# Two transformer blocks on one core: the retrieval's decode for four token tiles at once, with a selection by bits

## The chip, the cores and the metric

The kernel runs on one core of a Trainium2 chip. Its engines work side by side, each with a queue of its own in order: TensorE (PE, with its weight loads as PEld), VectorE (DVE), ScalarE (ACT), GpSimd (POOL) and SyncE (SP), which issues most transfers. The metric is the device time of one execution in microseconds; the median of the runs counts.

## The reference, cut to what matters

512 tokens of 1024 features pass two blocks of a transformer. The first has a mixer of attention and RWKV heads and a gated feed-forward network; the second has HGRN2 and retention heads and then PEER, a layer that retrieves its experts. The change touches PEER alone:

```
q = (h @ w_q).reshape(T, 8 heads, 2 halves, 128)
s = einsum('thpd,hpkd->thpk', q, sub_keys)          # 128 sub-keys for each (head, half)
top_s, top_i = top_k(s, 16)
cand = top_s[:, :, 0, :, None] + top_s[:, :, 1, None, :]
cand_idx = top_i[:, :, 0, :, None] * 128 + top_i[:, :, 1, None, :]
best_s, best_c = top_k(cand.reshape(T, 8, 256), 16)
expert_idx = take_along_axis(cand_idx.reshape(T, 8, 256), best_c, axis=-1)
gates = softmax(best_s, axis=-1)
out[t] = sum over the 128 chosen of gates * gelu(expert_u[idx] . h[t]) * expert_v[idx]
```

There are 128 x 128 experts, so an expert is a pair of sub-keys (i, j).

## The kernel before, in words

Products are exact in float32: each operand is split in a high and a low part, and a product is three TensorE passes (`mm3`). Weights come through a ring of tiles of 128 x 1024 (`_load` on SP's queue, `_split`: the high part is a ScalarE copy, L238, and the low part a subtraction, L241). While the retrieval and the gate matrix run, `pool_split` is 1 and all low parts are made on POOL. The ring splits three tiles ahead.

The instructions of each engine are put in order by a planner when the program is built, after a model of time; an engine then runs its own list strictly in that order and waits where an operand is late. Sections with `high_priority` are pulled forward, and `issue_after` holds a piece behind another.

PEER has four token tiles of 128 tokens. For the first three, all experts are computed: for each j, the product of the 128 rows (., j) of expert_u with the tokens (`expert_act`), gated and multiplied with expert_v. For tile 3, the chosen rows are gathered from DRAM by POOL's indirect DMA (`gather_rows`). The order of `peer` is:

- `retrieve`, for groups hp of two heads (four products c of a head and half each): the product with w_q (`gemm_fm`), ScalarE's copy q, the scores `psc` on TensorE, ScalarE's copy `sc`; then for each tile `top16` on VectorE (five instructions: eight largest, their places, replace, and again, 16 in all). After each pair of halves, POOL adds the candidates of a tile (`cand`, 64 + 48 columns of the pairs that can be chosen) and VectorE finds their best 16 (`bs`, their places `bc`). When the group's four products are through, `decode` runs once for each tile: softmax of the scores into `gate`, the place in `bc` taken apart into the two places a and b (shifts, masks, casts to float and a predicated copy for candidates from 64 on), and then the sub-key at that place. For the latter a table lookup is made of an equality with 0 to 15 (VectorE, L1306, 128 x 512), a product with the 16 sub-key numbers (POOL, L1307) and a sum (VectorE, L1308) into `sel`.
- the gates and sub-keys of the three dense tiles are transposed (`slots_T`), and `gate_matrix` builds each token's 128 x 128 matrix of gates from two one-hots, `ohA` (VectorE) and `ohB` (VectorE or POOL), with TensorE (`pg`) and a ScalarE copy, and writes it to DRAM (`gd`).
- 25 of the 40 early `expert_act` products (L264 to L266 with `acc`) stand in the program between retrieval and gate matrix, and the planner may place them in TensorE's gaps; the last 15 run among the gate matrix's steps. Then follows the loop over all 128 j.

Of the kernel before, what the change touches and what calls it, by code (L numbers as in the profile page):

```python
# [57 lines left out]
TILES = (3, 0, 1, 2)  # L58
# [31 lines left out]
def prep(inp):  # L90
    """Lays the inputs out; every array is a permutation, slice or stack of inputs, or depends on shapes alone."""
# [77 lines left out]
# ---------------------------------------------------------------- program  # L169
class Prog:  # L170
# [26 lines left out]
    def banks(self, spec):  # L197
        """spec: "bank name name; ..." """
# [24 lines left out]
    # ring of weight tiles  # L223
# [44 lines left out]
    def gemm_fm(self, X, M=128, bank="acc", parts=1):  # L268
        """one block of 128 output features x 512 tokens; X: list of (hi, lo) FM chunks"""
# [42 lines left out]
    def split(self, src, name):  # L312
        """FM f32 chunk in SBUF -> exact parts"""
# [8 lines left out]
    # constants  # L322
    def consts(self):
# [12 lines left out]
        self.iota16 = self.iota[:, 0:16]  # L336
        # derived per-channel vectors
# [13 lines left out]
        # lower bound: softmax over the two rows, first row  # L351
# [8 lines left out]
        # f = lb + (1 - lb) (tanh / 2 + 1/2) = tanh * c1 + c0  # L360
# [7 lines left out]
    def attn_consts(self):  # L368
        """constants of the first mixers only"""
# [18 lines left out]
    def first_loads(self):  # L388
        """tokens, the first gain and the first weights in the order of their use"""
# [29 lines left out]
    def rstd_of(self, ss, n, eps, w=1):  # L419
        """(ss / n + eps) ** -0.5 of a small tile"""  # L420
# [7 lines left out]
    def new_U(self):  # L428
        """8 FM chunks of exact parts"""
# [4 lines left out]
    def rstd_row(self, ss):  # L434
        """(sum + eps) ** -0.5 of the two scaled square sums of a row"""
# [6 lines left out]
    def square(self, x, ss):  # L442
        """sum of squares / D along the row"""
# [3 lines left out]
    def norm_tile(self, i, gb, banks=("C", "D"), ss=None):  # L447
        """rmsnorm of one token tile of self.X, into its columns of the FM chunks; ss: with its first square sum"""
# [24 lines left out]
    def norm_fm(self, gb):  # L473
        """rmsnorm of self.X as 8 FM chunks of exact parts"""
# [44 lines left out]
    # ------------------------------------------------------------ block 1  # L519
# [10 lines left out]
    def lat_part(self, U):  # L530
# [19 lines left out]
        # forget gates of the attention heads: rows 32..39  # L550
# [18 lines left out]
    def fox_proj(self, c, U):  # L569
        """queries, keys and values of two heads"""  # L570
# [84 lines left out]
    def rwkv_elem(self, c):  # L655
        """two heads of the RWKV group on 128 channels"""
# [5 lines left out]
        # decay  # L662
# [15 lines left out]
        # in-context rate  # L678
# [9 lines left out]
        # normalised key  # L688
# [16 lines left out]
        # gate and bonus  # L705
# [41 lines left out]
        # [b k] scaled to the end of their chunk, tokens on partitions  # L747
# [9 lines left out]
        # rows: even head (b; k), odd head: transposed from (k; b)  # L757
# [4 lines left out]
        # scores  # L762
# [18 lines left out]
        # values, tokens on partitions  # L781
# [9 lines left out]
    def rwkv_inv(self, e, g_, h):  # L791
        """(I - N)^-1 of two chunks by doubling"""
# [878 lines left out]
```

## Time and profile before

| | us |
|---|---|
| median of 3 runs | 3137.03 |
| the three runs | 3127.26, 3137.03, 3152.71 |
| span of the profiled execution | 3129.2 |
| TensorE busy in it | 2961.4 (95%) |
| VectorE busy | 1938.7 (62%) |
| ScalarE busy | 1228.4 (39%) |
| POOL busy | 1508.5 (48%) |

The profiled execution has no time of its own beside its span, from its first to its last instruction. Busy shares are means over stages of different kinds; the rows below cut the span into stages. In a row, `cuf<-cm,cuf` means that tile cuf is written from tiles cm and cuf, `128x512` is partitions by elements of each, and a line Lnnn is that of kernel.py. In a wait, the part behind `<-` is what ended it.

### The profile page before, as it was taken

The numbers are of one execution on the slowest core, as the hardware profiler recorded it, in microseconds if no ns is written. First come the engines' busy times: TensorE is split into PE (matmuls) and PEld (weight loads), VectorE is DVE, ScalarE is ACT, GpSimd is POOL, SyncE is SP. The second block draws the span as 40 slices with busy tenths as digits, with TensorE's granted clock in tenths as the row PEclk, the third lists the DMA queues.
The fourth block names the chain that finished last, engine by engine and source line by source line (L and its number), as shares of the span: only waits on it lengthen the run. The fifth ranks groups of instructions, "written<-read, shape, count | busy, mean of one in ns | idle before, by whom it ended". The sixth has DMA issues, their size and how long they took to land.

```text
span 3129.2 us, 40869 instructions
## 1 busy us (share of the span) xinstructions
PE 2961.4 (95%) x15129; PEld 2547.7 (81%) x15129; DVE 1938.7 (62%) x3421; ACT 1228.4 (39%) x1925; POOL 1508.5 (48%) x1150
## 2 busy tenths in 40 slices
PE   7999898999999999999999978888999999999998
PEld 6877787888878878888888868887888888888876
DVE  4247755443135653555423899997777777787788
ACT  5455644222243433444423324565333333333333
POOL 3222213222245652333323457866767677667665
PEclk9998999999999999999999989999999999999999
DMA  4120013333332213222333223446888988888886
GB/s 156 56 68 8 1 38 109 97 98 97 95 113 69 62 47 101 85 85 85 90 116 123 92 68 95 142 169 219 297 275 293 308 289 298 299 280 299 285 310 240
DMA packets 174359, 473.65 MB, mean 151 GB/s; under 512 B 15056, under 2 KB 64592, under 8 KB 172624
## 3 DMA queue, kind: packets, MB, share of 16 engines
q1 hardware_dynamic: 137296, 336.80, 33.8%
q0 software_dynamic: 36864, 134.23, 12.2%
q8 instruction: 120, 1.97, 0.3%
q14 instruction: 79, 0.65, 0.1%
HBM read 439.49 MB, written 31.46 MB: 151 GB/s over the span
## 4 chain that ended last, share of the span: by engine, by line
PE 69%; DVE 15%; DMA 7%; issue 5%; ACT 2%; POOL 1%; SPq 0%; DVEq 0%; POOLq 0%; ACTq 0%
PE acc L266 13%; PE acc L265 13%; PE acc L264 13%; DMA urow<-ev,ei 3%; PE A L266 3%; PE A L264 3%; PE A L265 3%; PE B L266 3%; PE B L265 3%; PE B L264 3%; DMA urow<-eu,ei 2%; PE pg L1377 2%; DVE lo L241 2%; PE i L804 1%; PE lev L981 1%
## 5 line engine op out<-in xcount | busy, mean ns | idle before, releaser
L241 POOL TENSOR_TENSOR lo<-raw,hi 128x1024 fp32r<-128x1024 f32 x278 | 689.6, 2481 | 912.9 <-ACT hi L238 875.8
L238 ACT ACTIVATE hi<-raw 128x1024 fp32r<-128x1024 f32 x501 | 529.3, 1057 | 1065.7 <-PE acc L265 441.4
L266 PE MATMUL acc<-u,lo 128*128 128x512 f32 (+3 forms) x2344 | 864.6, 369 | 39.2 <-DVE lo L241 21.2
L264 PE MATMUL acc<-u,hi 128*128 128x512 f32 (+3 forms) x2344 | 862.4, 369 | 15.0 <-ACT x L1392 6.3
L265 PE MATMUL acc<-u,hi 128*128 128x512 f32 (+3 forms) x2344 | 862.1, 368 | 0.7 <-DVE u L471 0.7
L266 PEld LDWEIGHTS acc<-u,lo 128*128 128x128 f32 (+1 forms) x2344 | 448.1, 191 | 96.2 <-DVE lo L241 27.6
L264 PEld LDWEIGHTS acc<-u,hi 128*128 128x128 f32 (+1 forms) x2344 | 447.8, 191 | 70.0 <-ACT eact L1392 6.7
L265 PEld LDWEIGHTS acc<-u,hi 128*128 128x128 f32 (+1 forms) x2344 | 448.3, 191 | 54.8 <-issue 2.7
L241 DVE TENSOR_TENSOR lo<-raw,hi 128x1024 fp32r<-128x1024 f32 x223 | 304.4, 1365 | 301.1 <-ACT hi L238 299.9
L1332 DVE SCALAR_TENSOR_TENSOR urow<-urow,h4row 128x1024 f32<-128x1024 f32 x128 | 201.5, 1595 | 109.2 <-DMA urow<-eu,ei 108.9
L1342 DVE SCALAR_TENSOR_TENSOR po<-urow,act,po 128x1024 f32<-128x1024 f32 x127 | 203.2, 1600 | 84.9 <-DMA urow<-ev,ei 83.5
L1324 POOL DMA_INDIRECT urow<-eu,ei x128 | 193.5, 1512 | 32.6 <-issue 19.0
L1324 POOL DMA_INDIRECT urow<-ev,ei x128 | 176.6, 1380 | 37.8 <-issue 18.2
L1403 ACT ACTIVATE wh<-wf 128x384 fp32r<-128x384 f32 x128 | 67.1, 525 | 272.3 <-PE D L265 243.5
L1368 DVE TENSOR_SCALAR ohA<-iota,slT 128x128 f32<-128x128 f32 x384 | 129.8, 404 | 0.9 <-PE pg L1377 0.7
L1377 PE MATMUL pg<-ohB,ohA 128*128 128x128 f32 x768 | 106.3, 280 | 25.0 <-DVE ohB L1374 12.5
L1377 PEld LDWEIGHTS pg<-ohB,ohA 128*128 128x128 f32 x768 | 97.4, 191 | 32.7 <-ACT gstage L1379 16.1
L1379 ACT ACTIVATE gstage<-pg 128x512 f32<-128x512 f32 x96 | 99.5, 1089 | 57.8 <-PE pg L1377 57.7
L1372 POOL TENSOR_SCALAR ohB<-iota,slT 128x128 f32<-128x128 f32 x144 | 98.2, 698 | 39.9 <-PE pg L1377 39.7
L266 PE MATMUL A<-hi,wl 128*128 128x512 f32 x256 | 95.8, 399 | 10.0 <-DVE wl L1404 9.9
L265 PE MATMUL A<-lo,wh 128*128 128x512 f32 x256 | 101.0, 395 | 0.8 <-POOL lo L241 0.8
L264 PE MATMUL A<-hi,wh 128*128 128x512 f32 x256 | 99.8, 390 | 0.6 <-ACT wh L1403 0.6
(539 smaller groups left out, 5395.9 us busy)
## 6 DMA issues: line engine op xcount, KB each, us to landing
raw<-ut SPq DMA_DIRECT2D x128, 512.0 KB
raw<-ev SPq DMA_DIRECT2D x128, 512.0 KB
raw<-w_ret SPq DMA_DIRECT2D x48, 512.0 KB
gd<-gstage SPq DMA_DIRECT2D x12, 2048.0 KB
gread<-gd SPq DMA_DIRECT2D x32, 768.0 KB
raw<-w_gu SPq DMA_DIRECT2D x44, 512.0 KB
raw<-w_hg SPq DMA_DIRECT2D x32, 512.0 KB
raw<-w_in SPq DMA_DIRECT2D x27, 512.0 KB
```

Source lines behind the costliest of these rows:

```text
L238: self.nc.scalar.activation(hi, raw, AF.Copy)
L241: r = eng.tensor_tensor(lo, raw, hi.bitcast(F32), op=ALU.subtract)
L264: mm(out, a[0], b[0], start=start, stop=False)
L265: mm(out, a[0], b[1], start=False, stop=False)
L266: return mm(out, a[1], b[0], start=False, stop=stop).ins
L1324: r = nc.gpsimd.indirect_dma_start(out=u, out_offset=None, in_=src, in_offset=bass.IndirectOffsetOnAxis(ap=ei[:, s:s + 1], axis=0))
L1332: nc.vector.scalar_tensor_tensor(u, u, 1.0, row, op0=ALU.mult, op1=ALU.mult, accum_out=act[:, s:s + 1])
L1342: nc.vector.scalar_tensor_tensor(o, u, act[:, s:s + 1], o, op0=ALU.mult, op1=ALU.add)
L1368: nc.vector.tensor_scalar(A4[:, r], self.iota, sl[:, 0, k + r:k + r + 1], sl[:, 2, k + r:k + r + 1], op0=ALU.is_equal, op1=ALU.mult)
L1372: nc.gpsimd.tensor_scalar(B4[:, r], self.iota, sl[:, 1, k + r:k + r + 1], None, op0=ALU.is_equal)
L1377: last = nc.tensor.matmul(p[:, r, :], A4[:, r], B4[:, r], start=True, stop=True)
L1379: nc.scalar.activation(st[:, :, q * 4:q * 4 + 4].rearrange("p j t -> p t j"), p, AF.Copy)
```

## The change

The tiles of the retrieval get a dimension for the four token tiles, and `decode` runs once for each group of two heads on all four: four times in place of sixteen. POOL's two candidate sums run on all four tiles at once as well; `top16` stays one call for each tile and product, now in the order 0 to 3. The place of a candidate stays an integer. The lookup no longer compares, multiplies and sums: the 16 sub-key numbers (`tif`, now cast by ScalarE) are halved step by step. ScalarE spreads the lower eight over the 16 slots (`mux`, 128 x 2048); VectorE then, for the bits 8, 4, 2 and 1 of the place, masks the bit and copies the upper half of what is left over the lower half where the bit is set. ScalarE copies what remains into `sel`. The gates of the gathering tile get a copy of their own (`gate3`), since the retrieval's tiles are freed. Comments and docstrings go too.

```diff
-                for i in TILES:
-                    self.top16(ts[i][:, c, :], ti[i][:, c, :], s[:, i, :], 128)
+                for i in range(4):
+                    self.top16(ts[:, i, c, :], ti[:, i, c, :], s[:, i, :], 128)
                 if c % 2:
-                    for i in TILES:
-                        t0, t1 = ts[i][:, c - 1, :], ts[i][:, c, :]
-                        cand = self.b("cand", [128, 112])
-                        nc.gpsimd.tensor_tensor(cand[:, 0:64].rearrange("p (a b) -> p a b", b=16),
...
-                        self.top16(bs[i][:, c // 2, :], bc[i][:, c // 2, :], cand, 112)
-            for i in TILES:
-                self.decode(i, hp, ti[i], bs[i], bc[i])
+                    t0, t1 = ts[:, :, c - 1, :], ts[:, :, c, :]
+                    cand = self.b("cand", [128, 4, 112])
+                    for o, a, nb in ((0, slice(0, 4), 16), (64, slice(4, 16), 4)):
+                        na = a.stop - a.start
+                        nc.gpsimd.tensor_tensor(cand[:, :, o:o + na * nb].rearrange("p i (a b) -> p i a b", b=nb),
+                                                t0[:, :, a, None].to_broadcast([128, 4, na, nb]),
+                                                t1[:, :, None, 0:nb].to_broadcast([128, 4, na, nb]), op=ALU.add)
+                    for i in range(4):
+                        self.top16(bs[:, i, c // 2, :], bc[:, i, c // 2, :], cand[:, i, :], 112)
+            self.decode(hp, ti, bs, bc)
+        self.gate3 = self.b("gate3", [128, 8, 16])
+        nc.scalar.activation(self.gate3, self.gate[:, 3], AF.Copy)
...
+        ab = self.b("ab", [128, 4, 2, 2, 16], U32)
+        tail, u, f = self.b("cm", B2, U32), self.b("cu", B2, U32), self.b("cuf", B2)
         TS(tail, bc, 64, None, op0=ALU.is_ge)
-        for w in range(2):
-            uf = []
-            for n in range(2):
-                u = self.b("cu", B3, U32)
...
-            nc.vector.copy_predicated(uf[0], tail, uf[1])
-            eq = self.b("eq", B4)
-            TT(eq, uf[0][:, :, :, None].to_broadcast(B4), self.iota16[:, None, None, :].to_broadcast(B4), op=ALU.is_equal)
-            nc.gpsimd.tensor_tensor(eq, eq, tif[:, :, w, None, :].to_broadcast(B4), op=ALU.mult)
-            nc.vector.tensor_reduce(self.sel[i][w][:, H, :], eq, axis=AX.X, op=ALU.add)
+        TS(u, bc, 2, None, op0=ALU.logical_shift_right)
+        nc.vector.tensor_copy(f, u)
+        TS(f, f, -12.0, None, op0=ALU.add)
+        nc.vector.tensor_copy(u, f)
+        TS(ab[:, :, :, 0, :], bc, 4, None, op0=ALU.logical_shift_right)
+        nc.vector.copy_predicated(ab[:, :, :, 0, :], tail, u)
+        u = self.b("cu", B2, U32)
+        TS(u, bc, 3, None, op0=ALU.bitwise_and)
+        TS(ab[:, :, :, 1, :], bc, 15, None, op0=ALU.bitwise_and)
+        nc.vector.copy_predicated(ab[:, :, :, 1, :], tail, u)
+
+        tif = self.b("tif", [128, 16, 16])
+        nc.scalar.activation(tif, ti.rearrange("p i c k -> p (i c) k"), AF.Copy)
+        w = self.b("mux", [128, 16, 16, 8])
+        nc.scalar.activation(w, tif[:, :, None, 0:8].to_broadcast([128, 16, 16, 8]), AF.Copy)
+        n = 8
+        while n:
+            bit = self.b("bit", [128, 16, 16], U32)
+            TS(bit, ab.rearrange("p i h two k -> p (i h two) k"), n, None, op0=ALU.bitwise_and)
+            B4 = [128, 16, 16, n]
+            nc.vector.copy_predicated(w[:, :, :, 0:n], bit[:, :, :, None].to_broadcast(B4),
+                                      tif[:, :, None, 8:16].to_broadcast(B4) if n == 8 else w[:, :, :, n:2 * n])
+            n //= 2
+        w = w.rearrange("p (i h two) k e -> p i h two k e", h=2, two=2)
+        for j in range(2):
+            nc.scalar.activation(self.sel[j][:, :, H, :], w[:, :, :, j, :, 0], AF.Copy)
...
-        P.open(eq1, "retrieve", "xs 10 gb keys q sc; eq 4 junk; ts 8; ti 8; bs 8; bc 8; wk 3; cand 3; tif 4; cm 4; cu 4; cuf 8; ef 1; gate 3; sel0 4; sel1 4")
+        P.open(eq1, "retrieve", "xs 10 gb keys q sc; mux 1; ts 2; ti 2; bs 2; bc 2; wk 3; cand 2; tif 1; ab 1; bit 2; cm 1; cu 2; cuf 1; ef 1; gate 1; sel0 1; sel1 1")
```

The softmax at the head of `decode` keeps its five instructions, on four tiles each. A number behind a tile's name in the last two lines is its count of buffers: the retrieval's tiles of a group now have two, those inside `decode` mostly one.

## Rows read from the trace of the kernel before

**Rows 1.** The page's first line.

```profile
span 3129.2 us, 40869 instructions
```

**Rows 2.** Four stages; columns: length, busy us and instructions by engine, clock, DMA share, GB/s.

```profile
1743.60:1862.00 118.40, 106.36 (x523) 90.94 (x522) 117.08 (x634) 36.39 (x57) 62.23 (x63) 0.94 0.24 72
1862.00:1979.00 117.00, 89.28 (x460) 86.19 (x460) 116.30 (x474) 42.49 (x58) 84.26 (x69) 0.90 0.29 86
1979.00:2162.00 183.00, 158.31 (x1118) 150.89 (x1117) 175.81 (x439) 117.95 (x126) 136.93 (x158) 1.00 0.48 177
2162.00:3129.00 967.00, 925.97 (x4511) 819.90 (x4509) 732.65 (x774) 326.74 (x456) 658.43 (x374) 0.99 0.85 288
```

**Rows 3.** Chain of waits by line, 1743 to 1985, then 1985 to 2165 us.

```profile
by line: DVE wk L1228 9.7%; DVE eq L1306 8.6%; DVE sel L1308 6.8%; DVE ti L1230 6.6%; DVE ti L1226 6.6%; DVE cuf L1304 5.3%; DVE cu L1298 4.8%; DVE ts L1225 4.8%; DVE ts L1229 4.7%; DVE cuf L1303 4.2%; DVE tif L1287 3.6%; DVE gate L1280 3.4
...
by line: PE pg L1377 32.8%; DVE ohA L1368 11.7%; DVE ohB L1374 11.0%; PE acc L266 10.9%; PE acc L264 10.8%; PE acc L265 10.8%; issue 8.3%; ACT gstage L1379 3.7%; ACT eact L1392 0.1%; ACTq L1379 0.0%
```

**Rows 4.** VectorE's groups by line, 1743 to 1980 us: busy us, mean ns; idle before.

```profile
L1306 DVE TENSOR_TENSOR eq<-cuf,iota 128x512 f32<-128x512 f32 x32 | 25.2, 822 | 0.0
L1308 DVE TENSOR_REDUCE sel<-eq 128x32 f32<-128x512 f32 x32 | 21.4, 672 | 0.6 <-POOL eq L1307 0.6
...
L1304 DVE COPY_PREDICATED cuf<-cm,cuf 128x32 f32<-128x32 uint32 x32 | 15.5, 488 | 0.0
...
L1298 DVE TENSOR_SCALAR cu<-bc 128x32 uint32<-128x32 uint32 x32 | 13.7, 450 | 0.0
L1303 DVE TENSOR_SCALAR cuf<-cuf 128x32 f32<-128x32 f32 x16 | 11.5, 721 | 0.0
L1300 DVE CAST cuf<-cu 128x32 f32<-128x32 uint32 x64 | 10.5, 206 | 0.0
L1287 DVE CAST tif<-ti 128x64 f32<-128x64 uint32 x16 | 10.0, 640 | 0.0
L1280 DVE TENSOR_TENSOR gate<-bs 128x32 f32<-128x32 f32 x16 | 9.6, 598 | 0.0
...
L1296 DVE TENSOR_SCALAR cu<-bc 128x32 uint32<-128x32 uint32 x32 | 8.7, 286 | 0.0
...
L1285 DVE TENSOR_TENSOR gate<-gate,gsum 128x32 f32<-128x32 f32 x16 | 7.1, 446 | 0.0
...
L1290 DVE TENSOR_SCALAR cm<-bc 128x32 uint32<-128x32 uint32 x16 | 5.1, 320 | 0.0
```

**Rows 5.** VectorE in order of time: start us, length us.

```profile
1893.21 0.16 DVE L1290 TENSOR_SCALAR cm<-bc 128x32 uint32<-128x32 uint32 x1
1893.29 0.26 DVE L1296 TENSOR_SCALAR cu<-bc 128x32 uint32<-128x32 uint32 x2
```

**Rows 6.** One line or tile: least, middle, largest ns; first and last start us.

```profile
L1306 DVE TENSOR_TENSOR eq<-cuf,iota x32: 668/682/2901, 1783.3 to 1971.9; 128x512 f32<-128x512 f32 x32
...
L1308 DVE TENSOR_REDUCE sel<-eq x32: 661/673/687, 1791.5 to 1977.3; 128x32 f32<-128x512 f32 x32
...
L1304 DVE COPY_PREDICATED cuf<-cm,cuf x32: 175/190/2429, 1779.8 to 1968.6; 128x32 f32<-128x32 uint32 x32
...
L809 DVE COPY_PREDICATED Tt<-cu,NT x16: 432/448/930, 243.8 to 403.2; 128x256 f32<-128x256 uint32 x16
```

**Rows 7.** POOL's and ScalarE's groups by line, 1743 to 1980 us.

```profile
L241 POOL TENSOR_TENSOR lo<-raw,hi 128x1024 fp32r<-128x1024 f32 x37 | 88.3, 2392 | 33.2 <-ACT hi L238 29.9 <-DMA raw<-w_q 3.3
L1307 POOL TENSOR_TENSOR eq<-eq,tif 128x512 f32<-128x512 f32 x32 | 46.9, 1478 | 32.0 <-DVE eq L1306 30.6 <-DVE gate L1285 1.4
...
L238 ACT ACTIVATE hi<-raw 128x1024 fp32r<-128x1024 f32 x35 | 37.0, 1056 | 112.9 <-PE acc L265 53.6 <-issue 28.3 <-POOL eq L1307 13.9
```

**Rows 8.** Waits, 1743 to 1980 us: total us, times, longest us.

```profile
ACT gate L1281 <- DVE gate L1280: 40.2, 10, 11.6
...
PE acc L266 <- POOL lo L241: 17.9, 4, 6.6
...
PE psc L1253 <- ACT q L1250: 7.8, 1, 7.8
```

More of the change, by code (lines that the diff above doesn't have):

```diff
@@ L57 @@
 RB = "acc ge wg; A i0; B i1; C pe gv wf ys; D gt ga lt"
-TILES = (3, 0, 1, 2)
 def shape_consts():
@@ L1239, in retrieve @@
             kt.append(s)
-        self.gate = [self.b("gate3" if i >= NDENSE else "gate", [128, 8, 16]) for i in range(4)]
-        self.sel = [[self.b(f"sel{w}", [128, 8, 16]) for w in range(2)] for i in range(4)]
+        self.gate = self.b("gate", [128, 4, 8, 16])
+        self.sel = [self.b(f"sel{w}", [128, 4, 8, 16]) for w in range(2)]
         for hp in range(4):
-            ts = [self.b("ts", [128, 4, 16]) for i in range(4)]
-            ti = [self.b("ti", [128, 4, 16], U32) for i in range(4)]
-            bs = [self.b("bs", [128, 2, 16]) for i in range(4)]
-            bc = [self.b("bc", [128, 2, 16], U32) for i in range(4)]
+            ts, ti = self.b("ts", [128, 4, 4, 16]), self.b("ti", [128, 4, 4, 16], U32)
+            bs, bc = self.b("bs", [128, 4, 2, 16]), self.b("bc", [128, 4, 2, 16], U32)
             for c in range(4):
@@ L1255, in retrieve, with decode @@
                 nc.scalar.activation(s, p, AF.Copy)
-                for i in TILES:
-                    self.top16(ts[i][:, c, :], ti[i][:, c, :], s[:, i, :], 128)
+                for i in range(4):
+                    self.top16(ts[:, i, c, :], ti[:, i, c, :], s[:, i, :], 128)
                 if c % 2:
-                    for i in TILES:
-                        t0, t1 = ts[i][:, c - 1, :], ts[i][:, c, :]
-                        cand = self.b("cand", [128, 112])
-                        nc.gpsimd.tensor_tensor(cand[:, 0:64].rearrange("p (a b) -> p a b", b=16),
-                                                t0[:, 0:4, None].to_broadcast([128, 4, 16]),
-                                                t1[:, None, :].to_broadcast([128, 4, 16]), op=ALU.add)
-                        nc.gpsimd.tensor_tensor(cand[:, 64:112].rearrange("p (a b) -> p a b", b=4),
-                                                t0[:, 4:16, None].to_broadcast([128, 12, 4]),
-                                                t1[:, None, 0:4].to_broadcast([128, 12, 4]), op=ALU.add)
-                        self.top16(bs[i][:, c // 2, :], bc[i][:, c // 2, :], cand, 112)
-            for i in TILES:
-                self.decode(i, hp, ti[i], bs[i], bc[i])
-    def decode(self, i, hp, ti, bs, bc):
+                    t0, t1 = ts[:, :, c - 1, :], ts[:, :, c, :]
[10 more added lines that the diff above has]
+        nc.scalar.activation(self.gate3, self.gate[:, 3], AF.Copy)
+    def decode(self, hp, ti, bs, bc):
         nc = self.nc
@@ L1278, in decode @@
         H = slice(2 * hp, 2 * hp + 2)
-        g = self.gate[i][:, H, :]
-        TT(g, bs, bs[:, :, 0:1].to_broadcast([128, 2, 16]), op=ALU.subtract)
+        g = self.gate[:, :, H, :]
+        B2 = [128, 4, 2, 16]
+        TT(g, bs, bs[:, :, :, 0:1].to_broadcast(B2), op=ALU.subtract)
         nc.scalar.activation(g, g, AF.Exp)
-        sm = self.t([128, 2], name="gsum")
+        sm = self.t([128, 4, 2], name="gsum")
         nc.vector.tensor_reduce(sm, g, axis=AX.X, op=ALU.add)
         nc.vector.reciprocal(sm, sm)
-        TT(g, g, sm[:, :, None].to_broadcast([128, 2, 16]), op=ALU.mult)
@@ L1286, in decode @@
-        tif = self.b("tif", [128, 2, 2, 16])
-        nc.vector.tensor_copy(tif, ti.rearrange("p (h two) k -> p h two k", two=2))
-        B3, B4 = [128, 2, 16], [128, 2, 16, 16]
-        tail = self.b("cm", B3, U32)
-        TS(tail, bc, 64, None, op0=ALU.is_ge)
-        for w in range(2):
-            uf = []
-            for n in range(2):
-                u = self.b("cu", B3, U32)
-                if w == 0:
-                    TS(u, bc, 4 - 2 * n, None, op0=ALU.logical_shift_right)
-                else:
-                    TS(u, bc, 15 - 12 * n, None, op0=ALU.bitwise_and)
-                f = self.b("cuf", B3)
-                nc.vector.tensor_copy(f, u)
-                uf.append(f)
-            if w == 0:
-                TS(uf[1], uf[1], -12.0, None, op0=ALU.add)
-            nc.vector.copy_predicated(uf[0], tail, uf[1])
-            eq = self.b("eq", B4)
-            TT(eq, uf[0][:, :, :, None].to_broadcast(B4), self.iota16[:, None, None, :].to_broadcast(B4), op=ALU.is_equal)
-            nc.gpsimd.tensor_tensor(eq, eq, tif[:, :, w, None, :].to_broadcast(B4), op=ALU.mult)
-            nc.vector.tensor_reduce(self.sel[i][w][:, H, :], eq, axis=AX.X, op=ALU.add)
+        TT(g, g, sm[:, :, :, None].to_broadcast(B2), op=ALU.mult)
@@ L1310, in gather_rows @@
+        w = w.rearrange("p (i h two) k e -> p i h two k e", h=2, two=2)
+        for j in range(2):
+            nc.scalar.activation(self.sel[j][:, :, H, :], w[:, :, :, j, :, 0], AF.Copy)
     def gather_rows(self, i, row):
         nc = self.nc
-        g, sel = self.gate[i], self.sel[i]
+        g = self.gate3
         e = self.S([128, 8, 16], name="ef")
-        nc.vector.scalar_tensor_tensor(e, sel[0], 128.0, sel[1], op0=ALU.mult, op1=ALU.add)
+        nc.vector.scalar_tensor_tensor(e, self.sel[0][:, i], 128.0, self.sel[1][:, i], op0=ALU.mult, op1=ALU.add)
@@ L1347, in slots_T @@
         nc = self.nc
-        g, sel = self.gate[i], self.sel[i]
         p = self.b("pslT", [128, 3, 128])
-        for w, a in enumerate((sel[0], sel[1], g)):
-            nc.tensor.transpose(p[:, w, :], a.rearrange("p a b -> p (a b)"), self.ident)
+        for w, a in enumerate((*self.sel, self.gate)):
+            nc.tensor.transpose(p[:, w, :], a[:, i].rearrange("p a b -> p (a b)"), self.ident)
         t_ = self.B([128, 3, 128], f"slT{i}", 1)
```

1 line of the change is left out of this document (removed).

## The prediction, made before the result was known

> **What bounds the kernel now.** I read the page first: the profiled execution spans 3129.2 us [rows 1]. Then I cut the span from the first scores to the end in four stages [rows 2]. The last one, 967 us of expert products, is TensorE's (926 us busy) and holds nothing that the change edits. The change lies in the first two, 1743.6 to 1979 us, the retrieval: there VectorE is busy 233.4 of 235.4 us while TensorE is busy 195.6 and gets a clock of 0.94 and 0.90. TensorE could have worked more there: it sat idle for 39.8 us, and the lower clock took another 118.4 x 0.06 + 117.0 x 0.10 = 18.8. In the third stage, the gate matrix, VectorE is busy 175.8 of 183.0 us and TensorE 158.3. So two stages out of four, 418 us, have VectorE as their tight engine, with TensorE not far behind. The chain of waits says the same [rows 3]: from 1743 to 1985 us every line that it names is VectorE's, with the equality, the sum and the predicated copy among the first six; from 1985 on TensorE takes over half of it, beside VectorE's one-hots.
>
> **What the decode costs now.** Its kinds of instruction in the retrieval are [rows 4]; the reductions and reciprocals of the gate sums, few and small, are left out before and after. Together: 25.2 + 21.4 + 15.5 + 13.7 + 11.5 + 10.5 + 10.0 + 9.6 + 8.7 + 7.1 + 5.1 = 138.3 us in 304 instructions. Durations overlap, though: an instruction of 160 ns is followed 80 ns later by the next one [rows 5], so one takes its duration less some 85 ns of VectorE. 304 x 0.085 = 25.8, which leaves 112.5 us. The other half of the stage, 233.4 - 112.5 = 121 us, is mostly the top-16 search, which stays as it is, instruction for instruction.
>
> How much of the 112.5 is work? The least and middle durations [rows 6] tell: a predicated copy of 32 columns takes 190 ns, but up to 2429; the equality 682, but up to 2901; the reduction never over 687. Undisturbed, 224 instructions of 32 columns take 0.175 - 0.085 each (20 us), 16 casts of 64 columns some 0.21 - 0.085 (2), 32 equalities 0.60 (19) and 32 sums 0.585 (19): 60 us. The other 53 us are holds: the longest durations end at what one weight split on POOL takes, 2392 ns [rows 7].
>
> **The change, part by part.**
>
> Decode on VectorE. For each of the four groups of two heads, with all four tiles in one instruction: two subtract-or-multiply, eight shifts, masks and casts, two predicated copies, all of 128 columns; four bit masks of 256; four selecting copies of 2048, 1024, 512 and 256 columns. From the 32- and 512-column rows a plain one costs 1.06 ns a column: 0.27 us at 128 and 0.41 at 256. For predicated copies the rows of 32 and 256 columns (190 and 448 ns) give 1.15 ns a column: 0.30 at 128, then 2.51 + 1.33 + 0.74 + 0.45 = 5.03. So 10 x 0.27 + 2 x 0.30 + 4 x 0.41 + 5.03 = 9.97 less 20 x 0.085 = 1.7, 8.3 a group, 33 in all, against 60. The 2048-column price is extrapolated over a factor of eight, into strided views; no row shows that.
>
> Holds. 20 instructions a group that can be held, 80 in place of 272 (the sums are not held). By instructions, 53 x 80 / 272 = 16 us, the low end. The high end is every one of the stage's 37 splits holding VectorE for its full length, 37 x 2.39 = 88. I take 22: POOL loses its 46.9 us of products, so what holds falls from 135 to 88 us, and decode falls from 60 / 181 to 33 / 154 of VectorE's undisturbed work; 53 x 0.65 x 0.65 = 22, nearer to the low end, since most splits already fall beside the search. The Trainium skill (SBUF — State Buffer, section "Who interferes with whom") states that a VectorE instruction with two SBUF inputs and a GpSimd one that reads SBUF exclude each other for a whole instruction, and that a reduction never does; this speaks against trading reductions for predicated copies. The trace agrees on both [rows 6]; taken at its worst here it is the rival of holds below.
>
> Sum on VectorE: 112.5 - (33 + 22) = 57 us less, so 178 us for the retrieval's 235. Bounds: 63 less, or 9 more.
>
> POOL. 32 products go: 46.9 us of work and 30.6 us in which POOL waited for their equalities [rows 7]. The 64 candidate sums become 16 wider ones. POOL is busy 62% of the retrieval, so its work alone is no limit; its blocked queue was: splits stood behind these products, and TensorE waited 17.9 us for split weights [rows 8]. That goes. Candidate sums now need all four tiles; VectorE has the next score block to search meanwhile, so I cost that at nothing; without that cover it is 8 waits of 1.3 us (448 columns at the product's 1478 / 512 = 2.9 ns).
>
> ScalarE. Twelve exponentials go. Four spreads of 2048 columns come (1056 ns for 1024 [rows 7] gives about 2.0 us each), with four casts of 256 columns, eight copies out and one for the gathering tile, which I put at a third of the 1056 each: 8 + 13 x 0.35, some 12.5 us. ScalarE is busy 79 of 235 us, so the work hides in its idle time. The waits are what counts. The spread must await the cast, and the copies out the last selecting copy on VectorE; weight casts, q and score copies queue behind these. The row nearest: ScalarE waited 40.2 us, 10 times, for the gate's subtraction, and TensorE stood once for 7.8 us behind it [rows 8]. Bounds for the new waits: 0 and the 12 x 7.8 of the slower rival. I take 10 us, a little over that one stall.
>
> No DMA is added, removed or moved, and SP's queue keeps its order. The tail after the last search is now one whole decode, 8 us plus a hold or two, where it was the last tiles' share of one; TensorE has early expert products to run there, and without these the tail would stand bare, some 10 us.
>
> **What TensorE lets through.** TensorE's work in the retrieval is 195.6 - 18.8 = 177 us at full clock, as much as 178 us could hold. At 90% (83% now, with half its stalls gone) it does 160 there, and 17 us of early expert products move into the gate stage: 158 + 17 = 175 us, which at 93% take 188 us instead of 183. That gives back 5.
>
> **Sum.** 57 - 10 - 5 = 42 us less: 3129.2 - 42 = 3087 for the span. The median of the three runs, 3137.0, is 7.8 above it (they lie between 3127 and 3153), and 3137 - 42 is 3095. I say 3091, between the two.
>
> **Rivals.**
> 1. Given back in the gate stage. If TensorE reaches only 75% in the shorter retrieval, it does 134 us there and 43 move on: 158 + 43 = 201 us at 93% are 216. Then 178 + 216 = 394 of 418, 24 gained. With the same 4 us for the median, here and below: 3109. For it: TensorE is within 10% of VectorE in both stages, and its order is fixed ahead. Against: its longest stalls come from POOL's queue, which gets free. Chance 0.20.
> 2. Holds. Every split meets a selecting copy, or these are dearer than 1.15 ns a column in strided views: 33 + 88 = 121 us, 9 more than now (3142), or, half way, 24 less, of which ScalarE's waits take 10: 3119. For it: one split every 4 us or so, and copies up to 2.5 us long. Against: now the splits and products, 135 us, make only 53 us of holds. Chance 0.12.
> 3. Slower: ScalarE's queue. All 12 groups of new waits (exponential, cast with spread, copies out) cost TensorE the 7.8 us that one does now: 94 us of stalls on 177 of work is 271 against 235, so 36 more: 3169. It decides from (235 - 177) / 12 = 4.8 us a wait, from where the retrieval is no shorter. For it: the exponentials' waits now average 4 us. Against: only one of ten reached TensorE. Chance 0.08.
> 4. The decode shrinks, but the batch does less than it says: the search waits for candidates of all four tiles, 8 x 1.3 us, and ScalarE's waits double to 20: 20 less gain, 3111. Chance 0.05.
>
> **How the numbers follow.** The forecast has 0.55, with its own range of 3070 to 3110: 63 less on VectorE and no new ScalarE wait, less the 5 of the gate stage, gives 3129 - 58 = 3071; 19 us lost beyond the forecast gives 3110. The range takes in rivals 1, 2 and 4 and the spread of the runs: 3066 to 3138. A measurement here tells about 1% (31 us) from no change, so faster is below 3106. Faster: 0.55 x 0.95 + 0.20 x 0.4 + 0.17 x 0.1 = 0.62. Slower: the third rival, 0.08. Within: 0.30.
>
> **What would show it.** Right: the selecting copies near 2.5, 1.3, 0.74 and 0.45 us where not held; VectorE's retrieval ending near 178 us after the first scores; no POOL product of 512 columns, and fewer waits of TensorE for POOL's splits; a gate stage of 183 to 192 us with TensorE above 90%; the last stage at 967 within 5. Wrong: selecting copies above 4 us; new ScalarE waits of over 5 us each with TensorE idle behind them; a gate stage above 205; or a last stage that changes.

## The result, and the profile after

The changed kernel takes 3095.3 us (median of 4 runs, 3093.7 to 3103.3) against 3135.9 for the kernel before on the same chip: 0.989 times, 95% interval 0.986 to 0.992. Measured a second time beside the experiments it was 0.987 (0.985 to 0.989). The forecast was 3091 us, 42 us less on the span; the profiled span fell by 37.3.

```profile
span 3091.9 us, 40508 instructions
```

The page's first line of the changed kernel; [rows 1] has that of before. Next its stages (columns as in [rows 2]), cut at the last copy of the transposed slots and at the last product of the gate matrix:

```profile
1742.20:1922.00 179.80, 159.24 (x807) 143.06 (x807) 174.69 (x876) 70.60 (x101) 85.23 (x46) 0.94 0.28 85
1922.00:2126.00 204.00, 188.89 (x1325) 184.32 (x1325) 167.15 (x426) 130.22 (x143) 152.41 (x168) 1.00 0.49 176
2126.00:3091.90 965.90, 919.31 (x4478) 815.38 (x4476) 726.17 (x768) 323.40 (x452) 659.60 (x369) 0.99 0.85 289
```

Cut in the same way, the kernel before has these two stages, and 962.2 us after them (its first cut lies 3 us behind that of [rows 2], and the last 5):

```profile
1743.60:1982.00 238.40, 198.64 (x999) 180.10 (x998) 236.38 (x1109) 80.64 (x118) 149.49 (x134) 0.92 0.27 79
1982.00:2167.00 185.00, 160.00 (x1132) 152.29 (x1131) 174.50 (x443) 119.35 (x127) 136.68 (x160) 1.00 0.47 175
```

So the retrieval is 58.6 us shorter, the gate matrix 19.0 longer, the last stage 3.7 longer, and the scores begin 1.4 earlier: 37.3 in all. TensorE does 159 us in the retrieval in place of 199 and 189 in the gate matrix in place of 160: work has moved, as the prediction said, but more of it.

VectorE's groups in the retrieval (busy us, mean ns; idle before) that answer to [rows 4]:

```profile
L1308 DVE COPY_PREDICATED mux<-bit,tif 128x2048 f32<-128x2048 uint32 x4 | 13.8, 3457 | 0.0
L1308 DVE COPY_PREDICATED mux<-bit,mux 128x1024 f32<-128x1024 uint32 x4 | 10.0, 2509 | 0.0
...
L1306 DVE TENSOR_SCALAR bit<-ab 128x256 uint32<-128x256 uint32 x16 | 8.4, 552 | 0.0
...
L1308 DVE COPY_PREDICATED mux<-bit,mux 128x512 f32<-128x512 uint32 x4 | 5.0, 1242 | 0.0
L1308 DVE COPY_PREDICATED mux<-bit,mux 128x256 f32<-128x256 uint32 x4 | 4.9, 1237 | 0.0
...
L1278 DVE TENSOR_TENSOR gate<-bs 128x128 f32<-128x128 f32 x4 | 3.9, 965 | 0.0
L1291 DVE CAST cu<-cuf 128x128 uint32<-128x128 f32 x4 | 2.7, 666 | 0.0
...
L1288 DVE TENSOR_SCALAR cu<-bc 128x128 uint32<-128x128 uint32 x4 | 0.9, 216 | 0.0
```

All kinds of the decode, with the smaller ones not shown, last 60.6 us (mean times count) in 80 instructions. Less 80 x 0.085 that is 53.8 us; the forecast was 55. For the kernel before the same count gives 143.8 - 25.8 = 118 us, and not the prediction's 112.5: the busy times of [rows 4] that it added up count the time in which two instructions of a group overlap only once (64 casts of 206 ns are 13.2 us, but busy 10.5), so taking 85 ns off each took that overlap off twice. From the start of each instruction to the start of the next, the two traces give 118.0 and 53.0 us. Least, middle and largest durations, answering to [rows 6]:

```profile
L1308 DVE COPY_PREDICATED mux<-bit,mux x12: 1215/1254/3317, 1791.3 to 1908.5; 128x1024 f32<-128x1024 uint32 x4, 128x512 f32<-128x512 uint32 x4, 128x256 f32<-128x256 uint32 x4
...
L1308 DVE COPY_PREDICATED mux<-bit,tif x4: 2450/3461/4456, 1786.9 to 1899.0; 128x2048 f32<-128x2048 uint32 x4
```

The 2048-column copy takes 2450 ns undisturbed (forecast 2.51) and up to 4456, 2.0 us more; one split on POOL takes 2.39 [rows 7]. The order of time shows such a hold, first POOL and then VectorE (start us, length us):

```profile
1870.81 6.96 POOL L240 TENSOR_TENSOR lo<-raw,hi 128x1024 fp32r<-128x1024 f32 x2
...
1871.09 4.45 DVE L1308 COPY_PREDICATED mux<-bit,tif 128x2048 f32<-128x2048 uint32 x1
```

The copy starts inside the first of two splits, and it ends 2.0 us later than undisturbed; the two splits together take 6.96 us in place of 2 x 2.39. So each engine holds the other. Last, the waits that answer to [rows 8]:

```profile
ACT sel L1313 <- DVE mux L1308: 37.4, 4, 12.0
...
PE psc L1250 <- ACT q L1247: 9.4, 4, 5.5
...
PE acc L263 <- ACT x L1396: 7.9, 2, 7.2
...
ACT gate L1279 <- DVE gate L1278: 6.1, 4, 1.9
...
PE pslT L1355 <- ACT sel L1313: 3.5, 1, 3.5
...
DVE bs L1223 <- POOL cand L1262: 0.7, 2, 0.3
```

In the kernel before, TensorE waited for ScalarE not only the 7.8 us of [rows 8], but for early activations too:

```profile
PE acc L264 <- ACT x L1392: 6.3, 1, 6.3
...
PE acc L264 <- ACT eact L1392: 5.7, 2, 4.8
```

POOL's wait for equalities is gone, and so is TensorE's wait for POOL's splits. The exponential's wait fell from 40.2 to 6.1 us, but ScalarE now waits 37.4 us in four pieces for the last selecting copies. TensorE stands 9.4 + 7.9 = 17.3 us behind its copies of q and its early activations; before it was 7.8 + 6.3 + 5.7 = 19.8. And the copies of the transposed slots, before and after (first and last start):

```profile
L1353 ACT ACTIVATE slT<-pslT x3: 482/482/492, 1971.9 to 1981.6; 128x384 f32<-128x384 f32 x3
```

```profile
L1357 ACT ACTIVATE slT<-pslT x3: 483/483/484, 1911.8 to 1921.7; 128x384 f32<-128x384 f32 x3
```

Before, the first of them runs while VectorE still decodes (its last sum starts at 1977.3 [rows 6]); now all three follow VectorE's last selecting copy, which starts at 1908.5.

### The profile page after: what moved, and what is told of

The parts are those of the page before. It is cut to its first block, busy times and chain, and to the rows that moved or that the text cites. A ratio compares the mean times of both kernels' runs of the same rounds, so it can differ in the third digit from the quotient of the medians.

```text
span 3091.9 us, 40508 instructions
## 1 busy us (share of the span) xinstructions
PE 2947.8 (95%) x15129; PEld 2541.4 (82%) x15129; DVE 1864.2 (60%) x3173; ACT 1228.7 (40%) x1924; POOL 1464.5 (47%) x1070
## 3 DMA queue, kind: packets, MB, share of 16 engines
q0 software_dynamic: 36864, 134.23, 12.4%
## 4 chain that ended last, share of the span: by engine, by line
PE 71%; DVE 13%; DMA 7%; issue 5%; ACT 2%; POOL 2%; SPq 0%; DVEq 0%; POOLq 0%; ACTq 0%
PE acc L265 14%; PE acc L264 14%; PE acc L263 14%; DMA urow<-eu,ei 3%; DMA urow<-ev,ei 3%; PE A L265 3%; PE A L263 3%; PE A L264 3%; PE B L265 2%; PE B L264 2%; PE B L263 2%; PE pg L1381 2%; PE i L802 2%; DVE lo L240 1%; PE lev L979 1%
## 5 line engine op out<-in xcount | busy, mean ns | idle before, releaser
L240 DVE TENSOR_TENSOR lo<-raw,hi 128x1024 fp32r<-128x1024 f32 x223 | 294.9, 1322 | 300.9 <-ACT hi L237 300.6
L1347 DVE SCALAR_TENSOR_TENSOR po<-urow,act,po 128x1024 f32<-128x1024 f32 x127 | 210.8, 1660 | 82.8 <-DMA urow<-ev,ei 81.3
L1329 POOL DMA_INDIRECT urow<-eu,ei x128 | 192.2, 1502 | 35.2 <-issue 18.2
L1383 ACT ACTIVATE gstage<-pg 128x512 f32<-128x512 f32 x96 | 99.0, 1106 | 60.3 <-PE pg L1381 59.7
L1372 DVE TENSOR_SCALAR ohA<-iota,slT 128x128 f32<-128x128 f32 x384 | 117.1, 370 | 2.4 <-ACT slT L1357 1.2
```

The lines of the kernel that those rows point to most:

```text
L240: r = eng.tensor_tensor(lo, raw, hi.bitcast(F32), op=ALU.subtract)
L1329: r = nc.gpsimd.indirect_dma_start(out=u, out_offset=None, in_=src, in_offset=bass.IndirectOffsetOnAxis(ap=ei[:, s:s + 1], axis=0))
L1347: nc.vector.scalar_tensor_tensor(o, u, act[:, s:s + 1], o, op0=ALU.mult, op1=ALU.add)
L1372: nc.vector.tensor_scalar(A4[:, r], self.iota, sl[:, 0, k + r:k + r + 1], sl[:, 2, k + r:k + r + 1], op0=ALU.is_equal, op1=ALU.mult)
L1383: nc.scalar.activation(st[:, :, q * 4:q * 4 + 4].rearrange("p j t -> p t j"), p, AF.Copy)
```

## Experiments

**What is compared.** The theory: the gain is VectorE's decode time in the retrieval, of which a part comes back in the gate matrix. The rivals: POOL's queue, freed of its products; ScalarE's waits; TensorE's own work, which would bound the two stages once VectorE is faster; and holds by POOL's splits. In the table, "decode" is VectorE's as counted above (mean times count, less 85 ns for each instruction), the stages are from one profile of each kernel in the cuts above, "TensorE" is its idle time in the retrieval and its busy time in the gate matrix, and the ratio is to runs of the kernel before on the same chip.

| | decode | retrieval + gate matrix | sum | TensorE | ratio (95%) |
|---|---|---|---|---|---|
| kernel before | 118.0 | 238.4 + 185.0 | 423.4 | 39.8, 160.0 | 1 |
| changed kernel | 53.8 | 179.8 + 204.0 | 383.8 | 20.6, 188.9 | 0.989 (0.986 to 0.992) |
| the same again (e0_after) | 53.7 | 180.6 + 203.0 | 383.6 | 20.5, 187.9 | 0.987 (0.985 to 0.989) |
| e1_batch_lookup | 64.3 | 206.9 + 182.0 | 388.9 | 12.3, 155.4 | 0.986 (0.981 to 0.991) |
| e2_select_per_tile | 90.7 | 209.4 + 197.0 | 406.4 | 31.7, 177.6 | 0.996 (0.993 to 0.998) |
| e3_batch_product_dve | 84.1 | 211.2 + 181.0 | 392.2 | 15.4, 155.3 | 0.991 (0.988 to 0.994) |
| e9_more_dve | 59.8 + 52.4 | 237.0 + 171.0 | 408.0 | 23.2, 142.0 | 0.998 (0.994 to 1.001) |
| e4_copyout_dve | 61.1 | 188.6 + 203.0 | 391.6 | 29.0, 187.9 | 0.989 (0.987 to 0.991) |
| e5_no_select | 14.1 | 139.8 + 220.0 | 359.8 | 8.9, 211.5 | 0.979 (0.977 to 0.981) |
| e8_halved_splits | 51.4 | 178.4 + 203.0 | 381.4 | 17.1, 187.7 | 0.986 (0.984 to 0.987) |
| e6_less_pe_after | 59.7 | 188.6 + 192.0 | 380.6 | 30.4, 170.9 | 0.989 (0.986 to 0.992) |
| e7_less_pe_before | 120.9 | 243.8 + 180.5 | 424.3 | 58.5, 153.9 | 1.000 (0.998 to 1.003) |
| e12_planes | 47.2 | 172.2 + 204.0 | 376.2 | 14.9, 188.8 | 0.984 (0.982 to 0.986) |
| e13_planes_halved | 43.9 | 169.0 + 204.0 | 373.0 | 12.4, 188.6 | 0.982 (0.980 to 0.985) |

The last stage varies between 950 and 978 us from profile to profile (997 in one, e7) with no edit in it; so the sum of the two stages tells small edits apart better than one span does. The two profiles of the changed kernel differ by 0.2 us in it.

**One half of the change alone.** e1 keeps the batch and undoes the selection; e3 does the same with the product on VectorE; e2 keeps the selection and undoes the batch.

```diff
 e1 (changed kernel's decode, lookup as before, on four tiles; one buffer for eq)
-        w = self.b("mux", [128, 16, 16, 8])
...
+        B4 = [128, 8, 16, 16]
...
+            eq = self.b("eq", B4)
...
+               self.iota[:, None, None, 0:16].to_broadcast(B4), op=ALU.is_equal)
...
+            nc.gpsimd.tensor_tensor(eq, eq, tw, op=ALU.mult)
+            nc.vector.tensor_reduce(self.sel[w][:, :, H, :].rearrange("p i h k -> p i (h k)"),
...
 e3 (as e1, but)
+            nc.vector.tensor_tensor(eq, eq, tw, op=ALU.mult)
 e2 (kernel before; decode for each tile with its own mux, 128 x 512)
+        w = self.b("mux", [128, 4, 16, 8])
```

> Batching alone: four tiles at once, but the lookup stays equality (VectorE), product (POOL), sum (VectorE), with one buffer for the table. VectorE theory (the gain is VectorE's decode time, of which two thirds reach the end): per group 14 instructions of 128 columns, one cast of 256, two equalities and two sums of 2048, about 12 us undisturbed, 49 in all, and some 20 of holds: 69 for the 112 of before and the 54 of the changed kernel. So 43 of 59 us saved, some 28 us less, ratio 0.991 (0.988 to 0.995). POOL theory (the gain is POOL's queue, free of products and of waiting for equalities): POOL's 47 us of products stay, in pieces of 6 us that each block the splits; no gain, ratio 0.998 to 1.005.

> The selection by bits alone: decode stays one call for each tile, 16 in all. VectorE theory: per call 12 instructions of 32 columns, four masks of 64 and four selecting copies of 512 to 64 columns, 3 us undisturbed, 48 in all, with 320 instructions that can be held: some 40 of holds, 88 for 112. 24 us saved on VectorE, some 15 at the end, less what 16 spreads and 32 copies out cost in ScalarE's queue: ratio 0.995 to 1.000. POOL theory: the products are gone as in the changed kernel, so nearly its whole gain: 0.989 to 0.992.

> As the batching alone, with the product moved from POOL to VectorE (eight of 2048 columns, 2.2 us each, 18 us more on VectorE). VectorE theory: 67 undisturbed and 16 of holds, 83 for 112: 29 saved, some 20 at the end, ratio 0.994 (0.991 to 0.997), no better than with the product on POOL. POOL theory: POOL is free, so as good as the changed kernel: 0.987 to 0.990, and better than with the product on POOL.

Stages of e1, then its groups on VectorE and POOL (busy us, mean ns; idle before):

```profile
1739.10:1946.00 206.90, 194.62 (x1028) 178.71 (x1027) 188.82 (x865) 73.28 (x103) 138.90 (x63) 0.98 0.33 97
1946.00:2128.00 182.00, 155.39 (x1102) 147.36 (x1101) 167.51 (x434) 118.39 (x124) 130.24 (x159) 1.00 0.46 171
```

```profile
L1305 DVE TENSOR_TENSOR eq<-cuf,iota 128x2048 f32<-128x2048 f32 x8 | 23.6, 2956 | 0.1
L1309 DVE TENSOR_REDUCE sel<-eq 128x128 f32<-128x2048 f32 x8 | 18.2, 2278 | 15.4 <-POOL eq L1308 15.2
```

```profile
L1308 POOL TENSOR_TENSOR eq<-eq,tif 128x2048 f32<-128x2048 f32 x8 | 36.9, 4609 | 23.3 <-DVE eq L1305 23.3
```

Then TensorE's waits in the retrieval, of e1 and of e2 (total us, times, longest):

```profile
PE acc L265 <- POOL lo L240: 8.6, 5, 3.8
PE psc L1250 <- ACT q L1247: 3.7, 1, 3.7
```

```profile
PE psc L1253 <- ACT q L1250: 12.2, 5, 5.2
PE acc L264 <- ACT x L1399: 11.3, 4, 4.8
PE acc L264 <- ACT eact L1399: 4.7, 2, 3.3
```

The batch alone takes 34.5 of the 39.6 us off the two stages, with POOL's products still there (36.9 us of them), and in the times it can't be told from the whole change. The selection alone takes 17.0, as the VectorE theory said, with its decode at 91 us (expected 88) although the products are gone. As the whole cause, POOL's queue falls by both. But VectorE's decode time isn't the whole either: those of e2 and e3 lie 7 us apart (90.7 and 84.1), and their sums 14. In e2 TensorE waits for no split, but 28 us behind ScalarE's queue; in e1 it waits 8.6 us for splits, in place of the 17.9 of [rows 8], and 3.7 behind ScalarE. The times of e1 and e3 lie at the good end of what the VectorE theory gave, or beyond it.

**VectorE's time by itself.** e9 adds time, e5 takes some away.

```diff
 e9
+NRED = 6
...
+        junk = self.b("rj", [128, 256])
+        for _ in range(NRED):
+            nc.vector.tensor_reduce(junk, w.rearrange("p x k e -> p (x k) e"), axis=AX.X, op=ALU.add)
 e5
-        while n:
...
-            TS(bit, ab.rearrange("p i h two k -> p (i h two) k"), n, None, op0=ALU.bitwise_and)
...
-            nc.vector.copy_predicated(w[:, :, :, 0:n], bit[:, :, :, None].to_broadcast(B4),
...
```

> The changed kernel with work added on VectorE: six reductions of 2048 columns a group that nobody reads, 24 in all, some 2.25 us each, 54 us, not held by POOL. VectorE theory: the retrieval grows by about 54 us and the gate matrix gives some 15 to 20 of it back, so 35 to 40 us more than the changed kernel: ratio 0.998 to 1.003. POOL theory: VectorE has room, at most 10 us more: 0.989 to 0.993.

> The changed kernel with the bit masks and the selecting copies left out (the sub-key taken is the first of the list): 39 us less on VectorE, and ScalarE's copies out wait for nobody. If VectorE's time still reaches the end at the half that the added reductions showed: 20 us less than the changed kernel, ratio 0.982 to 0.984. If TensorE now bounds the two stages: 8 us less at most, 0.986 to 0.989. If VectorE alone bounds them: 35 less, 0.977 to 0.979.

Stages of e9, then of e5:

```profile
1741.00:1978.00 237.00, 213.76 (x1124) 197.96 (x1123) 231.38 (x893) 92.86 (x130) 119.79 (x59) 0.96 0.32 94
1978.00:2149.00 171.00, 142.03 (x1007) 132.36 (x1006) 161.19 (x434) 112.40 (x116) 119.72 (x155) 1.00 0.45 170
```

```profile
1741.20:1881.00 139.80, 130.92 (x673) 115.55 (x672) 134.29 (x838) 60.46 (x87) 64.26 (x40) 0.98 0.29 87
1881.00:2101.00 220.00, 211.50 (x1457) 208.29 (x1456) 190.52 (x433) 140.07 (x154) 166.29 (x174) 0.99 0.49 178
```

Adding 58 us of VectorE's time (six less than the change took off) costs 24 us in the two stages, 0.4 of it, where 35 to 40 were expected; in time, 0.998 is the low end of what was expected. Taking 40 us away gives 24, 0.6 of it; in time, 0.979 touches the range named for VectorE alone, but beside the 0.987 of the changed kernel in the same rounds it is 26 us, as the stages have it. So VectorE's time still counts in the changed kernel: the retrieval moves by nearly the whole (57 us longer, 40 shorter), and the gate matrix goes the other way, 171 us in e9 and 220 in e5, as expert products move between the stages.

The retrieval of e9 is as long as that of the kernel before (237.0 and 238.4 us), and yet the two stages are 15 us shorter. TensorE stood idle for 39.8 us of the retrieval before, 17.9 of them waiting for POOL's splits [rows 8]; in e9 it stands for 23.2, and waits for no split. So more of its work is done there, and the gate matrix is 14 us shorter.

**TensorE's work.** e6 and e7 take the same work from TensorE in either kernel, 28 us at the rate that their expectations give.

```diff
+            if j < 10:
+                self.nc.tensor.matmul(p[:, :n], hi[:, s], H4[k][0][:, :n], start=k == 0, stop=k == 7)
+            else:
                 self.mm3(...)
```

> The changed kernel with less work on TensorE: the first ten of the forty early expert products make one pass of the three (the two corrections are left out), 160 matmuls of 384 columns fewer, about 0.173 us each, 28 us. If TensorE now limits the two stages beside VectorE, a good part comes back: 12 to 25 us, ratio 0.979 to 0.984. If VectorE alone limits them: at most 5 us, 0.986 to 0.988.

> The kernel before with the same 28 us of TensorE's work left out. If VectorE bounded the retrieval there, with TensorE idle 40 of 238 us, little comes back, at most 12 us, all of it in the gate matrix: ratio 0.996 to 1.000. If TensorE's own work bounded it: 20 to 28 us, 0.991 to 0.994.

Stages of e6:

```profile
1739.40:1928.00 188.60, 158.22 (x767) 140.32 (x766) 180.76 (x876) 77.45 (x111) 98.32 (x51) 0.91 0.31 95
1928.00:2120.00 192.00, 170.92 (x1206) 164.46 (x1205) 164.78 (x426) 123.20 (x133) 139.78 (x163) 1.00 0.47 174
```

Before the change nothing comes back, as expected. After it 3 us of 28 come back in the two stages and nothing in the times; that is against my expectation too. The gate matrix is 12 us shorter, but the retrieval 9 longer, with a clock of 0.91 in place of 0.94 and 6 us more of decode on VectorE. TensorE's idle time in the retrieval grows by 10 us in e6 (20.6 to 30.4) and by 19 in e7 (39.8 to 58.5). So TensorE being full is not what bounds the retrieval in either kernel: work taken from it there comes back as waiting.

**ScalarE's wait and POOL's holds.**

```diff
 e4
-            nc.scalar.activation(self.sel[j][:, :, H, :], w[:, :, :, j, :, 0], AF.Copy)
+            nc.vector.tensor_copy(self.sel[j][:, :, H, :], w[:, :, :, j, :, 0])
 e8
-            r = eng.tensor_tensor(lo, raw, hi.bitcast(F32), op=ALU.subtract)
+            for s in ((slice(0, 512), slice(512, 1024)) if self.pool_split else (slice(0, 1024),)):
+                r = eng.tensor_tensor(lo[:, s], raw[:, s], hi.bitcast(F32)[:, s], op=ALU.subtract)
```

> The changed kernel itself, for comparison on the same chip: ratio 0.989 to the kernel before, retrieval and gate matrix together some 384 us, as first measured.

> The changed kernel with the eight copies out of the selection on VectorE in place of ScalarE (some 1.5 us more on VectorE). In the changed kernel ScalarE waits 37.4 us for the last selecting copies, and TensorE stood 9.4 us for q and 7.9 us for early activations behind it. Queue theory: most of these 17 us go, retrieval and gate matrix 8 to 15 us shorter, ratio 0.984 to 0.987. VectorE theory alone: TensorE would have waited for VectorE anyway, at most 3 us, 0.988 to 0.990.

> The changed kernel with each weight split on POOL cut in two instructions of 512 columns, in retrieval and gate matrix. Hold theory: a hold lasts 1.2 us at most in place of 2.4, VectorE's decode loses 8 to 10 of its 20 us of holds, and one-hots in the gate matrix as much again; at the end 5 to 10 us less, ratio 0.985 to 0.988. Rival: what is held once for long is held twice for short, and POOL pays for 56 more instructions; no change or 3 us more, 0.988 to 0.991.

Waits in e4's retrieval (total us, times, longest):

```profile
ACT tif L1300 <- DVE ti L1228: 34.7, 4, 13.3
...
PE acc L263 <- ACT x L1396: 8.7, 2, 7.6
...
PE acc L263 <- ACT eact L1396: 7.3, 1, 7.3
PE psc L1250 <- ACT q L1247: 7.0, 1, 7.0
```

e4 missed: the wait for the selecting copies is gone, but ScalarE now waits 34.7 us for the next group's places (16.2 in the changed kernel), and TensorE stands 8.7 + 7.3 + 7.0 us behind it. The sum is 8 us longer; VectorE's decode is 7 longer too, of which the eight copies should be 1.5, the rest is in masks that were held more (883 ns on average, 552 in the changed kernel). In the times e4 can't be told from the changed kernel. Where ScalarE's list runs ahead of VectorE, the next instruction that needs VectorE took the wait over here. e8 shortens the decode by 2.4 us, not by 8: holds become shorter but not much fewer us. Its 2.4 us in the sum are more than two profiles of the changed kernel differ by, but the intervals of the times overlap, so the gain isn't shown in them.

**Short runs.** In the changed kernel the copies of 512 and 256 columns take about the same, 1.24 and 1.22 us, where the rows of before give 0.74 and 0.45. They work on runs of 2 and 1 columns in steps of 8.

```diff
-        w = self.b("mux", [128, 16, 16, 8])
+        w = self.b("mux", [128, 8, 16, 16])
...
-            nc.vector.copy_predicated(w[:, :, :, 0:n], bit[:, :, :, None].to_broadcast(B4), ...)
+            nc.vector.copy_predicated(w[:, 0:n], bit[:, None, :, :].to_broadcast(B4), ...)
```

> The changed kernel with the selection's table turned: the eight entries lie outermost, so that every selecting copy works on whole planes of 256 columns in place of runs of 4, 2 and 1 in steps of eight. In the changed kernel the copies of 1024, 512 and 256 columns take about 2.0, 1.24 and 1.22 us where undisturbed. Run theory (short runs cost): 1.33, 0.74 and 0.45 us here, 1.9 us a group and 7.7 us in all less on VectorE; at the 0.6 that the left-out copies gave back, 4 to 5 us less, ratio 0.985 to 0.987 and retrieval with gate matrix 377 to 381 us. Rival (they were held by POOL): the same durations as now, no change.

> The turned table together with weight splits on POOL cut in two, the two edits that the runs point to. If their gains add: 7 us less than the changed kernel, ratio 0.983 to 0.986; if they overlap, as the turned table alone.

The copies in e12 (least, middle, largest ns), two of them undisturbed in order of time, and the stages of e13:

```profile
L1309 DVE COPY_PREDICATED mux<-bit,mux x12: 426/768/3409, 1792.0 to 1902.2; 128x1024 f32<-128x1024 uint32 x4, 128x512 f32<-128x512 uint32 x4, 128x256 f32<-128x256 uint32 x4
...
L1309 DVE COPY_PREDICATED mux<-bit,tif x4: 2545/3574/4589, 1787.6 to 1895.1; 128x2048 f32<-128x2048 uint32 x4
```

```profile
1796.94 0.75 DVE L1309 COPY_PREDICATED mux<-bit,mux 128x512 f32<-128x512 uint32 x1
...
1799.16 0.43 DVE L1309 COPY_PREDICATED mux<-bit,mux 128x256 f32<-128x256 uint32 x1
```

```profile
1739.00:1908.00 169.00, 156.63 (x807) 141.00 (x806) 164.87 (x873) 69.19 (x101) 94.86 (x74) 0.96 0.30 90
1908.00:2112.00 204.00, 188.59 (x1327) 184.48 (x1326) 172.83 (x430) 129.78 (x143) 156.76 (x192) 1.00 0.48 178
2112.00:3062.20 950.20, 914.38 (x4477) 810.45 (x4475) 734.32 (x768) 323.49 (x452) 656.39 (x371) 1.00 0.86 293
```

In whole planes they take 0.75 and 0.43 us: what the forecast had. The copy of 1024 columns did not get shorter (2.01 us before the turn, 2.13 after it, at the same place); it was held, not slowed by its runs of four, so my expectation was wrong there. The changed kernel's trace shows it:

```profile
1833.49 2.79 POOL L240 TENSOR_TENSOR lo<-raw,hi 128x1024 fp32r<-128x1024 f32 x1 [1.77 <-ACT hi L237]
...
1835.42 1.98 DVE L1308 COPY_PREDICATED mux<-bit,mux 128x1024 f32<-128x1024 uint32 x1
```

The copy ends 1.12 us after the split, and in each of the four groups it is 1.11 to 1.13; in e12 it is 1.23 to 1.25. Decode falls by 6.6 us and the two stages by 7.6, more than the 4 to 5 expected. With the halved splits, decode and sum fall by another 3 us, to 373.0 us and 0.982 (0.980 to 0.985): the fastest kernel here, 10.8 us below the changed kernel in the two stages and 15 by the ratios 0.987 and 0.982, whose intervals don't touch (each against the kernel before on its own chip).

**All fourteen profiles together.** The gate matrix's length follows TensorE's busy time in it, 0.69 us for each us: 171 us for 142 (e9), 220 for 211.5 (e5), and a straight line misses none of the fourteen by over 1.1 us, e6 and e7 included, the only two that change TensorE's work by itself. VectorE does not set it: its busy time there fell from 174.5 to 167.2 us while the stage grew by 19. By this line, what TensorE can't do in the retrieval is paid at 0.69 behind it: a us off the retrieval is worth 0.31 at the end if TensorE was busy in it, and a us of TensorE's idle time inside the retrieval 0.69. For the change these two give 58.6 x 0.31 = 18.2 and 19.2 x 0.69 = 13.2 us; another 7.3 come from TensorE's own busy time, 10.5 us less in the two stages, mostly because the granted clock was below full for less time (0.92 for 238 us, then 0.94 for 180). That is 38.7 of the 39.6. For e1 the same sum gives 35 (measured 34.5) and for e2 17 (17.0).

## Why the prediction was right

- **VectorE bounds the two stages.** Right for the retrieval: e9 and e5 change VectorE's work alone, and its length goes along by nearly the whole; e7 shows that TensorE's amount does not count before the change. Not right for the gate matrix, whose length follows TensorE's work.
- **Decode 112.5 to 55 us.** The 55 is right, 53.8 was measured; the 112.5 was 118, by the overlap taken off twice (which makes 58 us of holds in it, not 53). So VectorE saved 64 us where the sum had 57. Inside the 53.8, the two small selecting copies cost 1.3 us a group more than priced by rows of whole tiles (short runs); plain instructions of 128 columns and masks of 256 cost 0.21 and 0.27 us, less than the 0.27 and 0.41 assumed. With the least durations seen, and 1.12 us for the 1024-column copy, which was never seen free, it is 34 us of work (forecast 33) and some 20 of holds (forecast 22, between 16 and 88).
- **The tail.** It grew, under cover as the prediction had it. VectorE's last decode instruction ends 234 us after the first search before, 168 after the change (forecast 178), 67 us less; the retrieval is only 58.6 shorter, since the copies of the transposed slots now all follow. TensorE is busy for all of the 15 us from 1911 to 1926.
- **ScalarE's queue, 10 us.** Too much: the sum took off 10 us for new waits, but TensorE stood 17.3 us behind ScalarE, and 19.8 before, of which the prediction read 7.8. The new waits did come, in place of the old ones. Against e1, which has no selecting copies and 3.7 us of such waits, they cost TensorE some 14 us, and so take back part of what the selection saves.
- **The gate matrix gives back 5 us.** Too small: it gave back 19. TensorE worked 159 us in the retrieval, 148 at full clock (0.94 of 180 us), where 160 was assumed; so 29 us of products moved, not 17. That TensorE would then be busy for 93% of the stage is right (188.9 of 204.0).
- **The sum.** The retrieval came out 12 us better than the 57 - 10 of the sum and the gate matrix 14 worse than its 5. That these nearly cancel is luck; the direction, and the two stages in which it happens, are not.
- **POOL.** Its wait for equalities and TensorE's 17.9 us of waiting for splits went, as forecast. The prediction gave this no price of its own; at 0.69 it is some 12 us. It does not take moving the products off POOL: with 8 products in place of 32, e1 gets half of it.
- **Rivals.** The first (given back in the gate matrix) came in part: 204 us, where it had 216, with TensorE at 83% of full work in the retrieval, between its 75% and the 90% assumed. Its ground, that TensorE is within 10% of VectorE in both stages, holds for the gate matrix alone; in the retrieval it is 16% (195.6 and 233.4 us). The holds stayed near their low end. The slower one needed 4.8 us of TensorE's time for each of twelve waits; it was 17.3 / 12 = 1.4. Of the fourth, the search waited 0.7 us for candidates.
- **Its own signs.** They were less sure than the total. As a sign of being right it named a gate matrix of 183 to 192 us: it was 204. As signs of being wrong it named a selecting copy above 4 us (4.46, held) and new ScalarE waits of over 5 us with TensorE idle behind them (four, of 9.4 on average): both came, and the time was near the forecast all the same.

What the prediction did not ask is which half of the change pays. The batch does, nearly all of it: 304 instructions become about 80, fewer of them meet a split, and each pays the fixed part of its duration once for four tiles. In the selection, what VectorE saves is for the most part lost again by TensorE's waits: 20.6 us of idle time in the retrieval, against 12.3 in e1.

## What to carry to other kernels

Where an engine is busy all through a stage, sum its instructions as start to start, and split that sum in work and holds by the least and the largest durations; the work and the holds of the changed decode then came out within 2 us. Add up durations for that (mean times count), not busy times, if you take the overlap off each instruction. Batching small VectorE instructions pays twice while POOL runs, by the fixed part of each and by the holds that it can meet. What one stage saves is not what the end sees: here 0.4 to 0.6 of VectorE's time, since the products that had filled the longer stage moved into the next, where each us of them cost 0.69. So look first at how long the engine that must do the moved work waits inside the stage: a us of that was worth about twice a us of the stage's length.

## What the hardware showed beside this

A predicated copy of float32 with runs of two or one columns in steps of eight took 4.8 ns a run (1.24 and 1.22 us for 256 runs), against 0.75 and 0.43 us on whole planes; runs of four columns, 16 bytes, cost nothing extra (1.12 us behind the end of the split, 1.24 on whole planes). Which of its streams pays, the one read or the one written, no run tells. The Trainium skill (SBUF — State Buffer, section "Door 1: The DMA port swizzle") has SBUF in lines of 16 bytes, where two accesses to a line are enough for full speed; the runs of four and of one agree, the runs of two do not, and there the measurement decides.
